# First mixer's modulation parts as column-tiled matmuls, gate row applied at the PSUM banks, negated attention scores

## The chip, the cores and the metric

The kernel runs on one core of a Trainium2 chip. The metric is the device time of one execution in microseconds (us), taken as the median of the runs. All inputs are fp32 and the result is held to fp32 accuracy. In this text PE is the matmul engine (TensorE), DVE is VectorE, ACT is ScalarE, POOL is GpSimd, and SP is the queue that issues the loads.

## What is computed

A trunk of two layers over 512 tokens of width 1024. Layer 0 mixes tokens with an mLSTM in chunks of 128 tokens, layer 1 with differential attention (8 heads, two score maps each). After each mixer comes a mixture of experts (16 experts, 2 chosen per token). Six modulation vectors per layer, `mod`, scale, shift and gate both halves:

```python
c_act = jax.nn.silu(c)
for l in range(DEPTH):
    mod = (c_act @ w_ada[l] + b_ada[l])[:, None, :]
    sh1, sc1, g1, sh2, sc2, g2 = jnp.split(mod, 6, axis=-1)
    h = _rms(x, norm1[l]) * (1.0 + sc1) + sh1
    y = _mlstm_mixer(h, ...) if l == 0 else _diff_attention(h, ...)
    x = x + g1 * y
    h = _rms(x, norm2[l]) * (1.0 + sc2) + sh2
    x = x + g2 * _grouped_moe(h, ...)

# inside _diff_attention, for a block of 128 queries
p = jax.nn.softmax(jnp.where(mask, q @ k.T * 64 ** -0.5, -jnp.inf), axis=-1)
a = p[:, :, 0] - lam * p[:, :, 1]

# at the end of either mixer: y = o @ w_out
```

## The kernel before

**Products.** A big product is three matmuls: the weight block is split into a rounded high part (ACT copy, L228) and the low part that is left (subtraction, L229), the activations likewise, and high x high, high x low and low x high are added in one PSUM bank. `split` puts the low part on VectorE. Only the strips named `qk0` (first strip of layer 0) and `b00` (first strip of layer 1) put it on GpSimd, by the last argument at the call in `strip`. Low parts live in two buffers.

**Modulation parts.** A part (l, j) is the product of the 1024 values of `cact` with a 1024x1024 block of `w_ada`, loaded as four chunks of 1 MB into the four buffers "raw", which the mixer's weights use too. Layer 0's parts 0 and 1 are made at the start by `ada_half` (matmuls, L326). During mixer 0 the six parts (0,2) to (0,5), (1,0) and (1,1) are made by `ada` off the matmul engine: ACT or VectorE scales the two halves of a chunk by the channel's value (L255, L257, L259), GpSimd adds what ACT scaled into the accumulator `acc` (L260), and at the end of a part `column_sums` turns the accumulator by eight transposes (L301), VectorE sums over the turned rows (L302) and adds the bias (L307). During mixer 1 the four parts (1,2) to (1,5) are made by `ada_rows`: four small matmuls per chunk, each with the channel values in one column of a 32-column group, side by side in one bank (L280, the tile `rowada`), evacuated into `acc` by ACT for a part's first chunk (L284) and by VectorE for the others (L286), and summed over rows by four narrow matmuls at the end of a part (`row_sums`, L312). An fp32 matmul is recorded as two.

**Output projection.** `out_proj` runs at the end of each mixer in two halves of two tokens' tiles (128 tokens each). For half 0 the four banks `po` are multiplied by the gate row `grow` (L499) and then added to the tokens `x` (L500). While half 0 runs, GpSimd multiplies each block of the still loaded weights `wo` by the gate row (L512), after its split, so that half 1 splits gated weights and only adds (L500).

**Attention.** Per block, head and map: scores `s` (L917); VectorE adds the mask and takes the row maximum (L920); VectorE multiplies that by -0.125 (L923); ACT takes exp(0.125 s - 0.125 max) with its sum (L924). Then reciprocals, the factor with lambda (L928), a scaling of the second map (L929), an addition to the first (L930), transposes `aT` (L939), and the product with v (L949). The normed rows `qrow` and `orow` come from VectorE (L891 to L897, L964) and are turned on the matmul engine (`qkT` L903, `oT` L976).

**Order.** Functions put steps off by `later`, and the framework's scheduler then orders the instructions of each engine on a modelled timeline, except those that `ordered` keeps in program order. Every engine works its list in order, and SP issues the loads in its own. `normed_T` squares a token tile at the start of a layer (ACT, L373), and VectorE (L366) and GpSimd (L367) make 1/rms from it. L1616 is the last addition of the experts' output to a token tile.

## Time and profile before

| what | value |
| --- | --- |
| median of 3 runs | 1228.6 us (1227.84 to 1230.41) |
| profiled execution, its own time | 1225.23 us |
| its span in the trace | 1223.4 us |
| mean granted matmul clock of it | 0.952 of full speed |
| busy: PE, DVE, ACT, POOL | 92%, 66%, 54%, 25% of the span |
| moved by DMA | 320.81 MB, 262 GB/s over the span |

The profiled execution is one run, 3.4 us below the median; some 2 us of its time lie outside the span. Mixer 0 takes about 30 to 285 us of the span, the experts of layer 0 up to some 580, mixer 1 up to some 920, the experts of layer 1 the rest. A window row lists, for a stretch, how long each engine was busy and in brackets how many instructions it had there, then the granted clock (1.00 is full speed, 0.50 half of it), the share of the DMA engines' time that was busy and the rate. A timeline row has the start, the duration, engine, line, operation and operands; "x8" means that eight instructions are merged, and square brackets give the idle time of the engine just before and what ended it. A matmul's duration is longer than the distance to the next matmul's start, since matmuls are pipelined, so costs on PE are read from start to start.

### The profile page before, as it was taken

The page shows a single profiled execution, that of the slowest core. Times are in us where ns is not written, and L with a number is a line of the kernel's source. Part 1 is how long each engine was busy: PE and PEld are TensorE (multiplying, and loading weights), DVE is VectorE, ACT ScalarE, POOL GpSimd, SP SyncE. Part 2 cuts the span into 40 slices and gives each one's busy share as a digit, 9 for nine tenths or more (in the row PEclk, how much of TensorE's full clock was granted, in tenths as well). Part 3 has the DMA queues.
Part 4 walks back from the last instruction along what each step waited for, and adds up shares of the span by engine and source line. Part 5 has one row for each costly group of instructions (what it writes and reads, how often), then busy time and mean ns, then how long its engine had stood idle before and what let it go on. Part 6 is the DMA issues. An engine that isn't in the chain of part 4 may idle for free.

```text
span 1223.4 us, 17320 instructions
## 1 busy us (share of the span) xinstructions
PE 1126.9 (92%) x5954; PEld 816.0 (67%) x5954; DVE 808.9 (66%) x1617; ACT 659.1 (54%) x1118; POOL 307.7 (25%) x245
## 2 busy tenths in 40 slices
PE   5999999988999999996899999978797999999976
PEld 3677777777787875332897877757586787774322
DVE  4566878887888995006856566675677899893024
ACT  3456675443788885112655555555553888883110
POOL 2555482462211111101211021223233211111100
PEclk8999999997999999998999999988896999999998
DMA  9788662195799999999124444411275899999994
GB/s 345 267 284 302 230 216 104 59 346 194 280 383 382 386 380 368 398 408 370 37 70 141 138 169 138 173 69 74 99 280 193 316 386 385 377 380 372 396 414 182
DMA packets 104172, 320.81 MB, mean 262 GB/s; under 512 B 12673, under 2 KB 25097, under 8 KB 103056
## 3 DMA queue, kind: packets, MB, share of 16 engines
q1 hardware_dynamic: 95120, 298.67, 65.8%
q0 software_dynamic: 8960, 20.99, 4.7%
q8 instruction: 49, 0.80, 0.3%
q14 instruction: 43, 0.35, 0.1%
HBM read 309.66 MB, written 20.97 MB: 270 GB/s over the span
## 4 chain that ended last, share of the span: by engine, by line
PE 70%; DMA 12%; DVE 11%; ACT 4%; issue 2%; POOL 1%; SPq 0%; DVEq 0%; POOLq 0%; ACTq 0%
PE pge L237 8%; PE pue L237 8%; PE pge L1339 6%; PE po L237 6%; DMA we<-in_moe_w_gu_dram 5%; DMA ada<-in_w_ada_dram 5%; PE py0e L237 4%; PE py1e L237 4%; PE pye L1366 3%; PE s L917 3%; PE pcf L1398 2%; PE o L949 2%; PE xTe L427 1%; PE rowada L280 1%; PE psr L1087 1%
## 5 line engine op out<-in xcount | busy, mean ns | idle before, releaser
L1339 PE MATMUL pge<-we,xfe 128*64 128x512 f32 x448 | 106.3, 616 | 19.2 <-DMA we<-in_moe_w_gu_dram 19.2
L260 POOL TENSOR_TENSOR acc<-acc,ada 128x1024 f32<-128x1024 f32 x30 | 80.8, 2694 | 54.8 <-ACT ada L259 22.2
L1348 DVE TENSOR_TENSOR acte<-acte,pge 128x256 f32<-128x256 f32 x14 | 5.9, 421 | 119.3 <-ACT acte L1347 119.3
L1311 POOL DMA_INDIRECT xg<-h2d,lstd x26 | 26.8, 1031 | 223.0 <-PE xTe L427 152.5
L1339 PEld LDWEIGHTS pge<-we,xfe 128*64 128x64 f32 x448 | 30.4, 141 | 74.4 <-issue 51.1
L367 POOL TENSOR_TENSOR qrs<-qrs,nhalf 128x4 f32<-128x4 f32 x32 | 35.5, 1111 | 154.9 <-DVE qrs L366 126.5
L1366 PE MATMUL pye<-we,aTe 128*64 128x512 f32 x224 | 50.6, 593 | 1.1 <-ACT aTe L1355 1.1
L259 ACT ACTIVATE ada<-ada,cact 128x1024 f32<-128x1024 f32 x30 | 33.8, 1145 | 31.0 <-DMA ada<-in_w_ada_dram 31.0
L924 ACT ACTIVATE p<-p,mx 128x128 f32<-128x128 f32 (+3 forms) x64 | 35.7, 559 | 23.7 <-DVE mx L923 23.6
L920 DVE CUSTOM_DVE_ANT_0 p<-s,maskW 128x128 f32<-128x128 f32 (+3 forms) x64 | 30.4, 487 | 26.6 <-ACT orow L951 14.3
L512 POOL TENSOR_TENSOR wo<-wo,grow 128x1024 f32<-128x1024 f32 x16 | 40.9, 2573 | 23.6 <-DVE wos102l L229 15.8
L1347 ACT ACTIVATE acte<-pge 128x256 f32<-128x256 f32 x14 | 5.4, 383 | 73.1 <-PE pge L1339 73.1
L917 PE MATMUL s<-kTb,qTb 64*128 64x128 f32 (+3 forms) x128 | 40.1, 503 | 2.9 <-DVE mx L920 2.2
L1366 PEld LDWEIGHTS pye<-we,aTe 128*64 128x64 f32 x224 | 16.0, 137 | 32.3 <-issue 29.6
L427 PE MATMUL xTe<-ident,xg 128*128 128x128 f32 x144 | 23.0, 290 | 5.8 <-POOL we L220 3.2
L1463 POOL DMA_INDIRECT yd<-yoe,lstd x12 | 14.7, 1227 | 52.0 <-ACT yoe L1558 51.3
L949 PE MATMUL o<-vb,aTs 128*128 128x128 f32 x160 | 26.1, 303 | 0.7 <-ACT aTs L941 0.7
L1378 ACT ACTIVATE yo<-pye,twins 128x512 f32<-128x512 f32 x8 | 5.5, 687 | 38.9 <-PE pye L1366 38.9
L367 POOL TENSOR_TENSOR ors<-ors,nhalf 128x2 f32<-128x2 f32 (+1 forms) x12 | 11.2, 930 | 58.8 <-DVE mx L923 39.5
L949 PEld LDWEIGHTS o<-vb,aTs 128*128 128x128 f32 x160 | 23.2, 214 | 3.0 <-ACT aTs L941 1.6
L1379 POOL DMA_INDIRECT yd<-yo,rows x8 | 8.0, 1001 | 65.7 <-ACT yo L1378 65.4
L427 PEld LDWEIGHTS xTe<-ident,xg 128*128 128x128 f32 x144 | 18.5, 149 | 8.2 <-issue 6.0
(2557 smaller groups left out, 3871.5 us busy)
## 6 DMA issues: line engine op xcount, KB each, us to landing
we<-in_moe_w_gu_dram SPq DMA_DIRECT2D x128, 1024.0 KB, 8.7
we<-in_moe_w_down_dram SPq DMA_DIRECT2D x64, 1024.0 KB, 8.9
ada<-in_w_ada_dram SPq DMA_DIRECT2D x48, 1024.0 KB, 5.5
we<-yd SPq DMA_DIRECT2D x8, 1024.0 KB, 18.3
wo<-in_a_w_out_dram SPq DMA_DIRECT2D x4, 1024.0 KB, 4.9
wo<-in_b_w_out_dram SPq DMA_DIRECT2D x4, 1024.0 KB, 4.9
x<-in_x_dram SPq DMA_DIRECT2D x4, 512.0 KB, 5.0
qk0w<-in_a_w_in_dram SPq DMA_DIRECT2D x2, 1024.0 KB, 14.7
```

What stands on the lines that cost most here:

```text
L237: T.matmul(ps, (xh, xh, xl)[i], w, start=first and i == 0, stop=last and i == 2)
L259: A.activation(raw[:, k], raw[:, k], AF.Copy, scale=cact[:, kt:kt + 1])
L260: G.tensor_tensor(acc, acc, raw[:, k], op=ALU.add)
L367: pows.append(G.tensor_tensor(r, r, nhalf[:, 0:ncol], op=ALU.pow))
L427: T.transpose(ps[:, k * P:(k + 1) * P], row[:, kt * P:(kt + 1) * P], ident)
L512: G.tensor_tensor(raw[:, k], raw[:, k], grow, op=ALU.mult)
L917: T.matmul(ps[:, 0:n], part(qTs, h)[q0:q0 + BHD, j * P:(j + 1) * P], part(kTs, h)[q0:q0 + BHD, 0:n], start=True, stop=True)
L920: V.tensor_tensor_reduce(p[:, 0:n], ps[:, 0:n], maskW[:, S - n:S], scale=1.0, scalar=NEG, op0=ALU.add, op1=ALU.max, accum_out=mx[:, cc:cc ...
L924: A.activation(p[:, 0:n], p[:, 0:n], AF.Exp, scale=0.125, bias=mx[:, cc:cc + 1], accum_out=mx[:, 2 + cc:3 + cc])
L949: T.matmul(po[:, 0:P], aT[:, kb * P:(kb + 1) * P], part(vs, h)[:, kb * P:(kb + 1) * P], start=kb == 0, stop=kb == j)
L1339: T.matmul(pgu[hf * CS:(hf + 1) * CS].rearrange("p (g c) -> p g c", g=2), x[:, kt], w[:, :, hf], start=kt == 0, stop=kt == NK - 1))
L1366: T.matmul(py[hf * CS:(hf + 1) * CS], aT[:, k, ch * CS:(ch + 1) * CS], w[:, 0, hf * 512:(hf + 1) * 512], start=ch + k == 0, stop=ch + k == 2))
```

## The change

- All of layer 0's later parts are made by `ada_rows`. `ada`, `column_sums` and `ada_sums` are gone, and one accumulator tile per layer serves all parts of that layer.
- The low parts of `qk0` and `b00` are made on VectorE like the others.
- The gate row is applied at the banks in both halves. The multiplication of the loaded weights on GpSimd is gone.
- The factor -0.125 goes into the column that scales the queries. The mask has the opposite sign, VectorE takes a minimum, exp gets scale -1, the separate multiplication of the extremum is gone, and the scaling and addition of the two maps are one instruction.
- The 1/rms of token tiles 2 and 3 at the start of layer 1 is issued after the last addition before it (`added`), and the last additions are kept in program order.

```diff
-    loads, last, act_last = [], [], []
+    loads, last, act_last, added = [], [], [], []
...
-    def ada(l, j):
...
-            for k in range(2):
-                kt = ch * 2 + k
-                if kt == 0:
-                    A.activation(acc, raw[:, k], AF.Copy, scale=cact[:, kt:kt + 1])
-                elif k == 0 and l == 0:
-                    V.scalar_tensor_tensor(acc, raw[:, k], cact[:, kt:kt + 1], acc, op0=ALU.mult, op1=ALU.add)
-                else:
-                    A.activation(raw[:, k], raw[:, k], AF.Copy, scale=cact[:, kt:kt + 1])
-                    G.tensor_tensor(acc, acc, raw[:, k], op=ALU.add)
...
     def ada_rows(l, j):
 
-        if j == 2:
+        if (l, j) in ((0, 2), (1, 2)):
             both[:] = [room[0].tile([P, D], F32, tag="acc", name=f"acc{l}{j}", bufs=room[1])]
...
-    def column_sums(dst, accs, name):
...
-    def ada_sums(l, j, acc):
...
     def modulation_parts(l):
...
-            yield from (ada_rows if l else ada)(i, j)
+            yield from ada_rows(i, j)
...
-        r = rstd_of(ss, 1, D, f"r{l}{t}")
+        with tc.issue_after(added[0].ins) if added and t > 1 else nullcontext():
+            r = rstd_of(ss, 1, D, f"r{l}{t}")
...
-                yield k0 + k, split(raw[:, k:k + a], a, n, f"{name}s{k0 + k}", G if name in ("qk0", "b00") else V)
+                yield k0 + k, split(raw[:, k:k + a], a, n, f"{name}s{k0 + k}")
...
-                    if half == 0:
-                        V.tensor_tensor(ps[t, n], ps[t, n], grow[:, cols], op=ALU.mult)
+                    V.tensor_tensor(ps[t, n], ps[t, n], grow[:, cols], op=ALU.mult)
                     V.tensor_tensor(xt[t][:, cols], xt[t][:, cols], ps[t, n], op=ALU.add)
...
-                if half == 0:
-                    G.tensor_tensor(raw[:, k], raw[:, k], grow, op=ALU.mult)
...
+            if nm == "q":
+                V.tensor_scalar(wc, wc, -0.125, None, op0=ALU.mult)
...
-            V.tensor_scalar(maskW[:, S - P:], maskW[:, S - P:], 0.0, NEG, op0=ALU.is_gt, op1=ALU.mult)
+            V.tensor_scalar(maskW[:, S - P:], maskW[:, S - P:], 0.0, -NEG, op0=ALU.is_gt, op1=ALU.mult)
...
-                    V.tensor_tensor_reduce(p[:, 0:n], ps[:, 0:n], maskW[:, S - n:S], scale=1.0, scalar=NEG,
-                                           op0=ALU.add, op1=ALU.max, accum_out=mx[:, cc:cc + 1])
+                    V.tensor_tensor_reduce(p[:, 0:n], ps[:, 0:n], maskW[:, S - n:S], scale=1.0, scalar=-NEG,
+                                           op0=ALU.add, op1=ALU.min, accum_out=mx[:, cc:cc + 1])
                     pr.append(p)
-                    V.tensor_scalar(mx[:, cc:cc + 1], mx[:, cc:cc + 1], -0.125, None, op0=ALU.mult)
-                    A.activation(p[:, 0:n], p[:, 0:n], AF.Exp, scale=0.125, bias=mx[:, cc:cc + 1],
+                    A.activation(p[:, 0:n], p[:, 0:n], AF.Exp, scale=-1.0, bias=mx[:, cc:cc + 1],
                                  accum_out=mx[:, 2 + cc:3 + cc])
...
-                V.tensor_scalar(p1[:, 0:n], p1[:, 0:n], mx[:, 5:6], None, op0=ALU.mult)
-                V.tensor_tensor(p0[:, 0:n], p0[:, 0:n], p1[:, 0:n], op=ALU.add)
+                V.scalar_tensor_tensor(p0[:, 0:n], p1[:, 0:n], mx[:, 5:6], p0[:, 0:n], op0=ALU.mult, op1=ALU.add)
...
-                        V.tensor_tensor(x, x, banks[t][hf], op=ALU.add)
+                        added[:] = [V.tensor_tensor(x, x, banks[t][hf], op=ALU.add)]
+                        ordered(added[0])
```

The matmul engine's list in the first strip of mixer 0, before. The tiles `qk0p` are that strip's banks, `psg` is the product for the gates, and `psada` the row sums of the parts made at the start:

```order
L479 MATMUL qk0p3_314<-ah0_139,qk0s2h_375 128x512
L480 MATMUL qk0p3_314<-al0_141,qk0s2h_375 128x512
L481 MATMUL qk0p3_314<-ah0_139,qk0s2l_376 128x512
L338 MATMUL psada01_403<-ones_f_95,row001_373 128x1 x4
L338 MATMUL psada01_403<-ones_f_95,row011_358 128x1 x4
L576 MATMUL psg_628<-ah0_139,wg_505 16x512
```

The same place after the change:

```order
L446 MATMUL qk0p3_314<-ah0_139,qk0s2h_375 128x512
L447 MATMUL qk0p3_314<-al0_141,qk0s2h_375 128x512
L448 MATMUL qk0p3_314<-ah0_139,qk0s2l_376 128x512
L304 MATMUL psada01_403<-ones_f_95,row001_373 128x1 x4
L304 MATMUL psada01_403<-ones_f_95,row011_358 128x1 x4
L259 MATMUL rowada020_544<-ada020_461,acc02_458 32x512 x4
L259 MATMUL rowada021_580<-ada021_495,acc02_458 32x512 x4
L446 MATMUL qk0p0_311<-ah1_140,qk0s4h_430 128x512
```

Two chunks of part (0,2) now stand between the matmuls of the strip; 22 more chunks stand between the matmuls from here to the beginning of the output projection.

VectorE's list at the end of layer 0's output projection, half 1, before. `po020` and `po021` are the banks of token tile 2, `po030` and `po031` those of tile 3, `guse00l` and `guse01l` low parts of the first expert's weights:

```order
L229 TENSOR_TENSOR guse00l_2665<-we0_1980,guse00h_2664 128x1024
L500 TENSOR_TENSOR x2_86<-x2_86,po020_2239 128x512
L500 TENSOR_TENSOR x2_86<-x2_86,po021_2240 128x512
L500 TENSOR_TENSOR x3_89<-x3_89,po030_2241 128x512
L229 TENSOR_TENSOR guse01l_2669<-we0_1980,guse01h_2668 128x1024
L500 TENSOR_TENSOR x3_89<-x3_89,po031_2242 128x512
```

The same place after the change:

```order
L229 TENSOR_TENSOR guse00l_2677<-we0_1996,guse00h_2676 128x1024
L465 TENSOR_TENSOR po020_2247<-po020_2247,grow0_1922 128x512
L465 TENSOR_TENSOR po021_2248<-po021_2248,grow0_1922 128x512
L466 TENSOR_TENSOR x2_86<-x2_86,po020_2247 128x512
L465 TENSOR_TENSOR po030_2249<-po030_2249,grow0_1922 128x512
L229 TENSOR_TENSOR guse01l_2681<-we0_1996,guse01h_2680 128x1024
L465 TENSOR_TENSOR po031_2250<-po031_2250,grow0_1922 128x512
L466 TENSOR_TENSOR x2_86<-x2_86,po021_2248 128x512
L466 TENSOR_TENSOR x3_89<-x3_89,po030_2249 128x512
L466 TENSOR_TENSOR x3_89<-x3_89,po031_2250 128x512
```

Four multiplications stand among the four additions, and three of the additions, one of them tile 2's second, now stand behind the low part `guse01l`.

VectorE's list at the start of layer 1, before. `ss` is a token tile's sum of squares, `r` its 1/rms, and `pcf` holds the experts' output:

```order
L366 TENSOR_SCALAR r11_5172<-ss11_5170 128x1
L1616 TENSOR_TENSOR x2_86<-x2_86,pcf20_5079 128x512
L1616 TENSOR_TENSOR x2_86<-x2_86,pcf21_5080 128x512
L366 TENSOR_SCALAR r12_5206<-ss12_5204 128x1
L1616 TENSOR_TENSOR x3_89<-x3_89,pcf30_5089 128x512
L1616 TENSOR_TENSOR x3_89<-x3_89,pcf31_5090 128x512
```

The same place after the change:

```order
L332 TENSOR_SCALAR r11_5184<-ss11_5182 128x1
L1580 TENSOR_TENSOR x2_86<-x2_86,pcf20_5091 128x512
L1580 TENSOR_TENSOR x2_86<-x2_86,pcf21_5092 128x512
L1580 TENSOR_TENSOR x3_89<-x3_89,pcf30_5101 128x512
L1580 TENSOR_TENSOR x3_89<-x3_89,pcf31_5102 128x512
L332 TENSOR_SCALAR r12_5218<-ss12_5216 128x1
```

The first step of tile 2's 1/rms now stands behind the two additions to tile 3.

## Rows read from the trace of the kernel before

**Rows 1.** The page: busy time and share of the span of the matmul engine

```profile
PE 1126.9 (92%) x5954; PEld 816.0 (67%) x5954; DVE 808.9 (66%) x1617; ACT 659.1 (54%) x1118; POOL 307.7 (25%) x245
```

**Rows 2.** Windows: stretch, length, busy time (instructions) per engine, clock, DMA share, GB/s

```profile
100.00:120.00 20.00, 19.12 (x88) 14.93 (x87) 13.94 (x18) 10.66 (x12) 10.26 (x5) 1.00 0.84 289
...
240.00:260.00 20.00, 13.50 (x67) 10.41 (x67) 19.93 (x22) 6.41 (x10) 17.48 (x8) 0.91 1.00 401
...
340.00:360.00 20.00, 20.00 (x93) 16.04 (x93) 18.31 (x18) 17.11 (x20) 2.85 (x3) 1.00 1.01 387
...
600.00:800.00 200.00, 199.17 (x1488) 164.06 (x1486) 126.24 (x482) 107.93 (x297) 38.80 (x36) 1.00 0.39 132
```

**Rows 3.** Timeline of PE in mixer 0: start us, duration us, line, operands

```profile
39.39 0.39 PE L479 MATMUL qk0p<-ah,qk0s2h 128*128 128x512 f32 x1
39.71 1.06 PE L326 MATMUL rowada<-ada,cpad 128*32 128x512 f32 x8
40.70 0.50 PE L480 MATMUL qk0p<-al,qk0s2h 128*128 128x512 f32 x1
```

**Rows 4.** Groups by line, PE: count, duration ns min/median/max, first and last start

```profile
L301 PE MATMUL psada<-ident,acc x48: 270/273/308, 80.2 to 238.3; 128*128 128x128 f32 x48
...
L312 PE MATMUL psada<-halves,acc x32: 165/252/372, 694.5 to 833.4; 128*128 128x2 f32 x32
```

**Rows 5.** The page's groups: count, busy us, mean ns, idle time before

```profile
L260 POOL TENSOR_TENSOR acc<-acc,ada 128x1024 f32<-128x1024 f32 x30 | 80.8, 2694 | 54.8 <-ACT ada L259 22.2
...
L512 POOL TENSOR_TENSOR wo<-wo,grow 128x1024 f32<-128x1024 f32 x16 | 40.9, 2573 | 23.6 <-DVE wos102l L229 15.8
```

**Rows 6.** Waits of PE, 40 to 240 us: total us, times, longest

```profile
PE n L704 <- DVE core L736: 2.6, 3, 1.6
PE v1p L455 <- DVE v1s2l L229: 1.1, 1, 1.1
PE qk1p L479 <- ACT qT L649: 0.8, 1, 0.8
PE psgT L585 <- DVE cs L302: 0.8, 1, 0.8
```

**Rows 7.** Waits of PE, 240 to 275 us

```profile
PE psrow L360 <- DVE swr L1030: 3.7, 1, 3.7
PE ht L427 <- DVE cs L302: 2.1, 1, 2.1
PE po L237 <- DVE wos010l L229: 0.7, 1, 0.7
```

**Rows 8.** Timeline of DVE: one low part in mixer 0, one in half 1

```profile
140.68 3.43 DVE L229 TENSOR_TENSOR v1s2l<-v1w,v1s2h 128x1024 fp32r<-128x1024 f32 x1
...
278.32 1.23 DVE L229 TENSOR_TENSOR wos017l<-wo,wos017h 128x1024 fp32r<-128x1024 f32 x1 [1.00 <-PE po L237]
```

**Rows 9.** Timeline of DVE and PE at half 1's end in layer 0

```profile
282.47 1.88 DVE L500 TENSOR_TENSOR x<-x,po 128x512 f32<-128x512 f32 x3 [0.60 <-PE po L237]
284.27 1.33 DVE L229 TENSOR_TENSOR guse01l<-we,guse01h 128x1024 fp32r<-128x1024 f32 x1
...
286.26 1.09 PE L1075 MATMUL x2T<-ident,x 128*128 128x128 f32 x8 [1.49 <-DVE x L500]
```

**Rows 10.** Timeline of DVE at the start of layer 1

```profile
582.22 0.15 DVE L366 TENSOR_SCALAR r<-ss 128x1 f32<-128x1 f32 x1 [1.27 <-ACT sq L373]
```

**Rows 11.** Waits of PE, 800 to 900 us

```profile
PE qkT L903 <- DVE mx L928: 4.7, 1, 4.7
PE oT L976 <- ACT o L978: 3.9, 3, 1.4
PE s L917 <- DVE mx L920: 2.2, 1, 2.2
PE aT L939 <- ACT o L978: 2.0, 1, 2.0
```

**Rows 12.** Timeline of POOL and DVE before two of these waits

```profile
814.11 5.24 POOL L512 TENSOR_TENSOR wo<-wo,grow 128x1024 f32<-128x1024 f32 x2
...
814.59 2.56 DVE L891 TENSOR_TENSOR qrow<-qrow,qrs 128x256 f32<-128x256 f32 x1
...
860.60 2.40 DVE L928 SCALAR_TENSOR_TENSOR mx<-mx,nlam 128x1 f32<-128x1 f32 x1
```

**Rows 13.** Window behind the last of these waits

```profile
864.50:871.33 6.83, 6.83 (x21) 3.97 (x20) 3.11 (x15) 4.59 (x17) 0.00 (x0) 0.50 0.01 4
```

More of the change, by code (lines that the diff above doesn't have):

```diff
@@ L243, in trunk @@
     mod = const.tile([P, 2, 6, NK], F32, name="mod")
-    def ada(l, j):
-        if room[2]:
-            room[2].pop()()
-        acc = room[0].tile([P, D], F32, tag="acc", name=f"acc{l}{j}", bufs=room[1])
-        for ch in range(4):
-            raw = load(wk(w_ada[l, ch * 256:(ch + 1) * 256, j * D:(j + 1) * D]), 2, D, f"ada{l}{j}{ch}")
-            for k in range(2):
-                kt = ch * 2 + k
-                if kt == 0:
-                    A.activation(acc, raw[:, k], AF.Copy, scale=cact[:, kt:kt + 1])
-                elif k == 0 and l == 0:
-                    V.scalar_tensor_tensor(acc, raw[:, k], cact[:, kt:kt + 1], acc, op0=ALU.mult, op1=ALU.add)
-                else:
-                    A.activation(raw[:, k], raw[:, k], AF.Copy, scale=cact[:, kt:kt + 1])
-                    G.tensor_tensor(acc, acc, raw[:, k], op=ALU.add)
-            if ch == 3:
-                room[2].append(lambda: ada_sums(l, j, acc))
-                later(3, lambda: room[2] and room[2].pop()())
-            yield
     def ada_rows(l, j):
-        if j == 2:
+        if (l, j) in ((0, 2), (1, 2)):
             both[:] = [room[0].tile([P, D], F32, tag="acc", name=f"acc{l}{j}", bufs=room[1])]
@@ L294, in ada_rows @@
             yield
-    def column_sums(dst, accs, name):
-        for i, acc in enumerate(accs):
-            ps = t_tile(f"{name}{i}")
-            for k in range(4):
-                T.transpose(ps[:, k * P:(k + 1) * P], acc[:, k * P:(k + 1) * P], ident)
-            V.tensor_reduce(dst[:, i], ps.rearrange("p (k n) -> p k n", k=4), axis=AX.X, op=ALU.add)
-    def ada_sums(l, j, acc):
-        cs = small.tile([P, 2, 4], F32, tag="cs", name=f"cs{l}{j}", bufs=2)
-        column_sums(cs, (acc[:, 0:512], acc[:, 512:]), f"psada{l}{j}")
-        V.tensor_tensor(mod[:, l, j], cs.rearrange("p a k -> p (a k)"), badc[:, l, j], op=ALU.add)
     def row_sums(l, j, acc):
```

## Prediction

> **What bounds the kernel now.** The page comes first, to see which engine is nearly always busy: the matmul engine, 92% of the span, with no other above two thirds [rows 1]. That is a mean over stages, so the windows by stage come next [rows 2]. Three kinds of stage are to be seen. In the body of mixer 0 (100 to 120 us is typical) PE is busy 19.12 of 20 us at the full granted clock, while VectorE and GpSimd are not full and the DMA engines have room. In the body of mixer 1 (600 to 800 us) PE is busy 199.17 of 200 us. In the experts (340 to 360 us) the DMA engines are full at 387 GB/s; their transfers start when the mixer in front has let its buffers go, so a mixer that ends later moves everything behind it by as much. The fourth kind is the exception: the ends of the two mixers, such as 240 to 260 us, where PE is busy only 13.50 us, VectorE 19.93 and GpSimd 17.48.
>
> Then come the waits of PE, to see who ends its idle time: in the body of mixer 0 all that is listed is small [rows 6], at the start of the output projection [rows 7] and at the end of attention [rows 11] single waits of 2 to 5 us stand. Last, the timeline around these, to see why the engine named was late [rows 8, 12].
>
> So the question is simple: the change takes work from GpSimd, ACT and VectorE, which wait, and gives the largest piece to PE, which doesn't. Against that stand the places where GpSimd's work holds up VectorE and through it PE.
>
> **Part 1: layer 0's parts by matmuls.** Removed are the additions on GpSimd (80.8 us busy [rows 5]), the scalings on ACT and VectorE, and the 48 transposes. Added are 6 x 4 = 24 chunks of eight matmul records each, their evacuations, and six row sums. The price of a chunk on PE is in the trace, since the start-up uses the same form: in the middle of the qk0 strip a run of eight starts at 39.71 and the next matmul at 40.70, so 0.99 us, while the strip's own matmuls around it start without a break [rows 3]. The record's own 1.06 us includes the pipelined end. I take 1.05, between them: 24 x 1.05 = **25.2 us**, all in stages where PE has no idle time to put it in. The row sums are 6 x 8 = 48 short records against 48 transposes [rows 4], each about as long as the other (252 against 273 ns): nothing, within 1 us either way. The evacuations (24 of them) are far fewer than the removed scalings and turned sums on the same two engines, and lie beside matmuls in a window where VectorE is busy 13.94 and ACT 10.66 of 20 us; I cost them at nothing. If that cover failed, a late evacuation holds its bank and with it the next chunk, some tenths of a us each; 0 to 3 us in all goes into the range.
>
> What comes back in the body of mixer 0 is at most the waits that depend on VectorE or ACT. The low part v1s2l took 3.43 us while GpSimd was adding, another low part of the same size with GpSimd idle 1.23 us [rows 8]; its wait (1.1) goes, the one on the turned sums (0.8) goes since these are removed, and of the 2.6 on `core` and the 0.8 on qT I give back half [rows 6], with about 0.9 from smaller ones like them: together **-4.5 us** (0 to -7).
>
> The Trainium skill ("SBUF — State Buffer", section "SBUF: two separate sides") says that VectorE and GpSimd lock a shared pair of ports for a whole instruction and the loser blocks. The trace agrees with the 3.43 against 1.23 us, and the rule would make GpSimd's removed work a gain for VectorE; it says nothing of PE, where this sum is made.
>
> **Part 2: gate row at the banks.** It removes 16 multiplications on GpSimd, 40.9 us [rows 5], and adds two multiplications for each of the two tokens' tiles in half 1, four per layer.
>
> At layer 0's output projection GpSimd is in a row of eight of these while the waits of 3.7, 2.1 and 0.7 us stand [rows 7]. The first two hang on VectorE steps that are late in the same stretch where VectorE is busy 19.93 of 20 us. With GpSimd quiet, and the turned sums gone, I take all 6.5 us as gone, and 1 us more because the clock falls for a while behind them (0.91 on average in that window [rows 2]): **-7.5 us** (-3 to -9). What is late next there is PE itself.
>
> At the end of attention the same thing is seen more sharply. From 814.11 GpSimd does two multiplications, and the step on `qrow` that starts on VectorE in that time lasts 2.56 us; PE waits 4.7 us for this chain. The step on `mx` at 860.60 lasts 2.40 us, with waits of 2.2 and 2.0 us around it [rows 11, 12]. Without GpSimd these steps cost some tenths, so I take 4.2 of the 4.7 and 4.0 of the 4.2. Behind the last wait the granted clock is at 0.50 (1.2 GHz) for 6.83 us with PE busy all through [rows 13]; at 2.4 GHz that work takes half, -3.4. Together 11.6. The `oT` waits (3.9 us) come from a chain between ACT and PE that the change does not touch, and stay; and a step that is no longer late may show another behind it, so I take **-10 us** (-5 to -13).
>
> The price stands at the end of half 1. Before, the last addition to tile 3 is behind three additions and a low part, all on VectorE without a break from 282.47, and PE already waits 1.49 us for it [rows 9]. Four multiplications of about 0.62 us each (an addition's share of the 1.88 us for three) join the list ahead of it; none has idle time to go into, except where a bank is finished early. 4 x 0.62 = 2.5 per layer, **+5 us** for both (0 to +7), since the router and all experts are behind these tiles.
>
> **Part 3: the rest.** At the start of layer 1 the 1/rms of tile 2 waited 1.27 us for the square on ACT with tile 3's additions queued behind it [rows 10]; afterwards they go first. That is **-1 us** (-2.5 to 0, the end of the chain being the square of tile 3). The low parts of qk0 and b00 on VectorE are six instructions of 1.23 us [rows 8] in places where VectorE waits for loads or matmuls: nothing (-1 to +1). The fewer steps per score map shorten VectorE's list, but between 600 and 800 us PE is busy 199.17 of 200 us [rows 2], so there is nothing to give back: 0 (-1 to 0; at the end of attention it is in the -10).
>
> **The sum**, against the profiled execution: +25.2 - 4.5 - 7.5 - 10 + 5 - 1 = **+7.2 us**, 1225.2 to 1232.4. That execution lies 3.4 us below the median of three; the same difference on the median gives 1228.6 + 7.2 = 1235.8, rounded **1236 us**. With the terms off by a few us in either direction: 1230 to 1242.
>
> **The rivals.**
>
> 1. *Faster: the waits at the mixers' ends go as a whole.* One mechanism: GpSimd's multiplications are what makes VectorE late, and without them PE runs through. Then go 7 us in the body, 9 in layer 0's projection, and in attention all four waits (12.8) with three low-clock stretches like the one at 864.5 (about 3.4, 1.7 and 1.7), so 19.6; the banks' multiplications cost 1 per layer. 25.2 - 7 - 9 - 19.6 + 2 - 1 = -9.4, **1219 us**. It decides from gains of 25.2 + 2 on. For it: three of the four engines lose work. Against: the `oT` waits hang on ACT. Chance 0.14.
> 2. *Faster: PE has room.* If a busy share of 96 to 100% overstates PE because matmuls are pipelined, chunks slip in between others. By the weight loads, busy 14.93 of 20 us [rows 2], 5.07 us would be free there, and the chunks need about 2.5 (25.2 over some 200 us); part 1 then costs nothing and the total is 7.2 - 25.2 = -18, **1211 us**. Against it stands the start of the next matmul, moved by the full 0.99 us [rows 3]. Chance 0.07. The Trainium skill ("Perfetto Trace Analysis", section "Identifying the Most-Contended Engine") holds matmul busy time to be no measure of headroom and points to the weight loads' busy share instead, which speaks for this rival.
>
> 3. *A wash.* Gains as in the forecast's better halves (-5, -8, -12), and the tail costs 2: 25.2 - 25 + 2 - 1 = +1, **1230 us**. Chance 0.14.
> 4. *Slower still: VectorE and the raw buffers become the bound.* A chunk now keeps its raw buffer until PE's ordered place for it, and the next strip's load on SP is queued behind; with four buffers, a chunk that waits some us for PE makes a strip's weights late. If that costs 0.5 us for each of 16 chunks of the body, and the gains are at their low ends (-2, -5, -7), the total is 25.2 + 8 - 14 + 5 = +24, **1253 us**. For it: loads took their place in a mixer whose DMA share is already 0.84 [rows 2]. Chance 0.10.
>
> That the change doesn't do what it says is no case with a chance of its own: the order shows the chunks in PE's list and the GpSimd steps gone.
>
> **Chances.** Forecast 0.55, rivals 0.14, 0.07, 0.14 and 0.10. About 0.2% (2.5 us) is what a measurement of this kernel can tell from no change, so same is 1226.1 to 1231.1. Faster: rivals 1 and 2, 0.21. Same: rival 3 and a corner of the forecast, 0.16. Slower: the rest, 0.63. For 8 in 10 the range takes in the forecast and the wash, reaches down into rival 1, half of it, and up into the beginning of rival 4: 1219 to 1247.
>
> **What the next profile would show.** Right: eight-record groups `rowada` some 1.05 us apart from the next matmul in 40 to 240 us, mixer 0 ending some 13 to 18 us later (25.2 - 4.5 - 7.5 + 2.5 = +15.7 when the experts of layer 0 begin), mixer 1 shorter by 6 to 10, no GpSimd multiplication at 234 or 814 us, VectorE's steps there at tenths of a us, PE's wait for `x` at the end of half 1 grown from 1.5 to about 4 us. Wrong: mixer 0 ending less than 10 us later (PE had room, or the stalls were worth more than listed), new waits of PE on DMA for strips (rival 4), or the clock at 0.50 around 816 to 871 us as before although GpSimd is quiet, which would mean that the `oT` chain sets that stretch.

## The result

The changed kernel takes 1243.97 us (median, 1238.86 to 1247.11), the kernel before 1229.47 us beside it. The ratio is 1.0115, with a 95% interval of 1.0075 to 1.0155: slower by 14.5 us. The direction was forecast, and the time lies in the range of 1219 to 1247; the amount is twice the +7.2 of the sum, so that the median lies 8 us above the 1236 that was forecast and outside its narrower 1230 to 1242. The profiled execution took 1245.97 us (span 1244.0), 2.0 above its median, while the one of before lies 4.2 below its own. So the two traces differ by 20.7 us where the medians differ by 14.5, and some 6 us of that is the spread of single executions. More on the spread below.

The page of the changed kernel, busy time and share of each engine, answering to [rows 1]:

```profile
PE 1160.9 (93%) x6146; PEld 822.8 (66%) x6146; DVE 741.8 (60%) x1532; ACT 628.5 (51%) x1092; POOL 169.8 (14%) x193
```

VectorE lost 67 us of work, GpSimd 138 and ACT 31; PE gained 34. The windows of the changed kernel, columns as in [rows 2]:

```profile
100.00:120.00 20.00, 20.00 (x100) 13.76 (x100) 7.76 (x12) 6.30 (x8) 0.00 (x0) 1.00 0.62 210
260.00:280.00 20.00, 18.07 (x95) 14.33 (x93) 15.17 (x23) 9.62 (x13) 6.62 (x6) 1.00 1.03 419
```

The body of mixer 0 is now PE from end to end. The start of the output projection, which lies some 20 us later, is no longer a hole: 18.07 busy where 13.50 were. A chunk, on PE's timeline, answering to [rows 3]:

```profile
99.79 0.39 PE L423 MATMUL v0p<-v0s2h,al 128*128 128x512 f32 x1
100.11 1.06 PE L259 MATMUL rowada<-ada,acc 128*32 128x512 f32 x8
101.11 0.50 PE L421 MATMUL v0p<-v0s2h,ah 128*128 128x512 f32 x1
```

1.00 us from start to start. Over layer 0's 192 records, each taken to the start of the matmul behind it, this sums to 26.2 us, 1.09 per chunk, with one wait of 0.4 us in it.

To see where the 20 us of the trace arise, I follow four points of the program. The first matmul of the first expert in layer 0 and in layer 1 (the two times in the first row), and the first matmul of mixer 1 (the first time in the second), before:

```profile
L237 PE MATMUL pge<-guse00h,xh0e x2: 793/794/794, 310.1 to 945.0; 128*128 128x512 f32 x2
...
L454 PE MATMUL b00p<-b00s0h,bh x16: 277/282/421, 588.3 to 602.3; 128*128 128x256 f32 x16
```

and after:

```profile
L237 PE MATMUL pge<-guse00h,xh0e x2: 793/794/794, 328.0 to 962.1; 128*128 128x512 f32 x2
...
L421 PE MATMUL b00p<-b00s0h,bh x16: 277/282/582, 608.3 to 622.0; 128*128 128x256 f32 x16
```

| point | later by (us) | forecast |
| --- | --- | --- |
| first expert, layer 0 | 17.9 | 15.7 |
| mixer 1 begins | 20.0 | 14.7 |
| first expert, layer 1 | 17.1 | 7.2 |
| end of the span | 20.6 | 7.2 |

Mixer 0 is off by two. Mixer 1 was to become 7.5 us shorter and is 2.9 shorter, which is below the 6 to 10 that the prediction named as a sign of being right. The rest is missing behind both mixers, where the experts were taken as merely shifted. The waits of PE at the end of mixer 1 (815 to 945 us), columns as in [rows 11], with `x2T` for the turned token tiles:

```profile
PE oT L940 <- ACT o L942: 3.8, 3, 1.5
PE x2T L1039 <- DVE x L466: 3.5, 2, 3.0
```

The same wait for the token tile in the kernel before (797 to 925 us):

```profile
PE x2T L1075 <- DVE x L500: 1.5, 1, 1.5
```

All three waits that the forecast took as gone are gone (4.7 + 2.2 + 2.0), the `oT` waits stand as forecast, and the wait for the token tile has grown from 1.5 to 3.5. Of the low clock at the end of attention, 27.3 us in four stretches between 816 and 878 us before, 13.7 remain: 10.2 at the `oT` waits (846.16 to 856.40) and 3.4 (887.12 to 890.53). So a sign that the prediction named for being wrong came true for the stretch at the `oT` chain, but most of the gain arrived. It was given back by what comes after it. VectorE's timeline at that place in the changed kernel, answering to [rows 9], which show the same place of layer 0:

```profile
928.55 1.23 DVE L229 TENSOR_TENSOR guse00l<-we,guse00h 128x1024 fp32r<-128x1024 f32 x1 [1.10 <-PE po L237]
930.37 1.30 DVE L465 TENSOR_TENSOR po<-po,grow 128x512 f32<-128x512 f32 x2 [0.59 <-PE po L237]
931.58 0.68 DVE L466 TENSOR_TENSOR x<-x,po 128x512 f32<-128x512 f32 x1
932.17 0.69 DVE L465 TENSOR_TENSOR po<-po,grow 128x512 f32<-128x512 f32 x1
932.77 1.91 DVE L229 TENSOR_TENSOR guse01l<-we,guse01h 128x1024 fp32r<-128x1024 f32 x1
934.61 0.68 DVE L465 TENSOR_TENSOR po<-po,grow 128x512 f32<-128x512 f32 x1
935.21 1.86 DVE L466 TENSOR_TENSOR x<-x,po 128x512 f32<-128x512 f32 x3
```

From 930.37 to 937.07 there is no break. Of tile 2 the second half and of tile 3 everything is finished behind a low part that belongs to the experts. By the order of the list the first of the last three additions is tile 2's second half, and it is this that PE waits 3.0 us for: PE goes on at 935.94, and tile 3 costs it no wait any more. Within the wait, at 934.90, its granted clock falls to 1.2 GHz (0.50). Windows of the low clock at this place, changed kernel and kernel before:

```profile
934.90:969.04 34.14, 26.18 (x114) 23.36 (x115) 23.94 (x95) 9.88 (x16) 9.10 (x10) 0.50 0.37 135
```

```profile
925.94:946.42 20.48, 13.75 (x65) 12.76 (x66) 14.61 (x76) 3.90 (x6) 6.85 (x7) 0.50 0.38 142
```

Before, PE is back at 2.4 GHz 1.4 us after the first expert's first matmul (946.42 against 945.0); now 6.9 us after it (969.04 against 962.1). The experts' first matmuls run at the low clock in between.

### The profile page after: what moved, and what is told of

Read it like the earlier page. It is cut to its first block, busy times and chain, and to the rows that moved or that the text cites. A ratio compares the mean times of both kernels' runs of the same rounds, so it can differ in the third digit from the quotient of the medians.

```text
span 1244.0 us, 17483 instructions
## 1 busy us (share of the span) xinstructions
PE 1160.9 (93%) x6146; PEld 822.8 (66%) x6146; DVE 741.8 (60%) x1532; ACT 628.5 (51%) x1092; POOL 169.8 (14%) x193
## 4 chain that ended last, share of the span: by engine, by line
PE 80%; DMA 8%; DVE 7%; ACT 2%; issue 1%; POOL 1%; SPq 0%; DVEq 0%; POOLq 0%; ACTq 0%
PE pge L237 8%; PE pue L237 8%; PE po L237 7%; PE pge L1303 6%; PE py0e L237 4%; PE py1e L237 4%; PE rowada L259 3%; DMA we<-in_moe_w_gu_dram 3%; PE pye L1330 3%; PE s L883 2%; DMA b00w<-in_b_w_in_dram 2%; PE pcf L1362 1%; PE xTe L394 1%; PE o L913 1%; DMA ada<-in_w_ada_dram 1%; PE psr L1051 1%
## 5 line engine op out<-in xcount | busy, mean ns | idle before, releaser
L1303 PE MATMUL pge<-we,xfe 128*64 128x512 f32 x448 | 106.7, 618 | 19.9 <-DMA we<-in_moe_w_gu_dram 19.9
L259 PE MATMUL rowada<-ada,acc 128*32 128x512 f32 x320 | 45.5, 604 | 0.4 <-PE psada L304 0.2
L265 DVE TENSOR_TENSOR acc<-acc,rowada 128x512 f32<-128x512 f32 x30 | 20.5, 684 | 22.8 <-PE rowada L259 22.8
L333 POOL TENSOR_TENSOR rs<-rs,nhalf 128x2 f32<-128x2 f32 x8 | 5.6, 696 | 193.0 <-DVE rs L332 184.5
L913 PE MATMUL o<-vb,aTs 128*128 128x128 f32 x160 | 24.2, 287 | 1.2 <-ACT aTs L905 1.2
L1362 PE MATMUL pcf<-yo,self 64*128 64x512 f32 x96 | 21.7, 598 | 2.3 <-DVE yo L1336 2.3
L915 ACT ACTIVATE orow<-o,mx 128x128 f32<-128x128 f32 x32 | 11.3, 362 | 23.3 <-PE o L913 23.3
## 6 DMA issues: line engine op xcount, KB each, us to landing
qk0w<-in_a_w_in_dram SPq DMA_DIRECT2D x2, 1024.0 KB, 14.7
```

The source lines that it names most:

```text
L259: T.matmul(ps[at:at + 32], cp[:, ch * 2 + k], raw[:, k, hf * 512:(hf + 1) * 512], start=True, stop=True)
L333: pows.append(G.tensor_tensor(r, r, nhalf[:, 0:ncol], op=ALU.pow))
L913: T.matmul(po[:, 0:P], aT[:, kb * P:(kb + 1) * P], part(vs, h)[:, kb * P:(kb + 1) * P], start=kb == 0, stop=kb == j)
L1303: T.matmul(pgu[hf * CS:(hf + 1) * CS].rearrange("p (g c) -> p g c", g=2), x[:, kt], w[:, :, hf], start=kt == 0, stop=kt == NK - 1))
L1362: ordered(T.matmul(banks[hf], sel[at, t], yo[at], start=first, stop=last))
```

## The experiments

Eleven kernels ran, for three questions: what the parts cost (1, 2, 4), what the gate row gains and gives back (3, 5 to 8), and which version is better than both kernels (4, 7, 9 to 11). Every ratio is against runs of the kernel before on the same chip, whose median was 1228.3 to 1228.7 us.

**1. The parts alone.** The kernel before, with only this:

```diff
-        if j == 2:
+        if (l, j) in ((0, 2), (1, 2)):
...
-            yield from (ada_rows if l else ada)(i, j)
+            yield from ada_rows(i, j)
```

> The kernel before, with layer 0's six later modulation parts made as column-tiled matmuls and nothing else changed. Theory (PE is full, chunks are paid in full): 24 chunks at the 1.09 us that the changed kernel shows, +26, less 4 to 8 us for waits of PE on VectorE that go in the body of mixer 0 with GpSimd's additions: 1247 to 1251 us against 1229.5. Rival (PE has room, or the additions on GpSimd were a large hidden cost): below 1240 us. Layer 1 should be as before, within 2 us.

Measured: 1248.17 us, ratio 1.0159 (1.0132 to 1.0187), +19.9 us. The first expert of layer 0 starts 22.1 us later and layer 1 adds nothing, since the one of layer 1 starts 21.9 later:

```profile
L237 PE MATMUL pge<-guse00h,xh0e x2: 792/792/792, 332.2 to 966.9; 128*128 128x512 f32 x2
```

Of the waits in 40 to 240 us this is the whole list (7.6 us before, its larger ones in [rows 6]):

```profile
PE rowada L280 <- PE psada L338: 0.9, 1, 0.9
PE s L685 <- ACT core L707: 0.6, 1, 0.6
PE qk0p L480 <- DVE wck L834: 0.3, 1, 0.3
PE ht L427 <- DVE h2l L430: 0.3, 1, 0.3
```

PE was full, and it pays for the chunks in full. GpSimd's additions were hidden but for the 5.5 us of waits that are gone. In the projection of layer 0, where GpSimd still multiplies the weights, the waits did not go with the parts and their turned sums. They are one wait now (240 to 330 us; the 5.3 us end at 276 us, the other 1.5 stand at the end of half 1 as before), against 6.5 in [rows 7]:

```profile
PE x2T L1075 <- DVE x L500: 6.8, 2, 5.3
```

**2. Half of the parts.** As in 1, for three of the six parts:

```diff
-        if j == 2:
+        if (l, j) in ((0, 5), (1, 2)):
...
-            yield from (ada_rows if l else ada)(i, j)
+            yield from (ada_rows if l or (i, j) in ((0, 5), (1, 0), (1, 1)) else ada)(i, j)
```

> The kernel before with three of layer 0's six later modulation parts, (0,5), (1,0) and (1,1), made as column-tiled matmuls, 12 chunks, and the other three as before; nothing else. Theory (a chunk is paid in full wherever it stands): half of what all six cost, 12 x 1.09 = 13 less some 2 to 4 us of waits, so 1237 to 1240 us against 1228.3. Rival (there is room on PE for some chunks and the last ones are the dear ones, or the first ones): below 1233 or above 1244 us.

Measured: 1240.09 us, ratio 1.0096 (1.0059 to 1.0133), +11.8. Twelve chunks cost 11.8 where twenty-four cost 19.9; half of that lies inside the interval. No room shows up for the first ones, and the last are not dearer within this interval.

**3. The gate row at the banks alone.** The kernel before, with this:

```diff
-                    if half == 0:
-                        V.tensor_tensor(ps[t, n], ps[t, n], grow[:, cols], op=ALU.mult)
+                    V.tensor_tensor(ps[t, n], ps[t, n], grow[:, cols], op=ALU.mult)
...
-                if half == 0:
-                    G.tensor_tensor(raw[:, k], raw[:, k], grow, op=ALU.mult)
```

> The kernel before with the gate row applied at the banks in both halves and the multiplication of the weights on GpSimd gone; nothing else changed. Theory (the negated scores, the low parts of the first strips and the order at the start of layer 1 are worth 1 us together): within 2 us of the run that has all of the change but the parts, so 1220 to 1224 us. Rival (those small edits carry a gain or a loss of their own): 4 us or more away from it.

Measured: 1220.47 us, ratio 0.9938 (0.9919 to 0.9957), -7.8 us. Its waits of PE between 790 and 930 us, the two longest in sum:

```profile
PE oT L973 <- ACT o L975: 3.8, 3, 1.4
PE x2T L1072 <- DVE x L499: 3.5, 2, 3.0
```

These head the list as in the changed kernel, with neither the parts nor the other edits in it: the waits of 4.7, 2.2 and 2.0 were GpSimd's multiplications, and the longer wait for `x` is the multiplications at the banks. The same points as above:

```profile
L237 PE MATMUL pge<-guse00h,xh0e x2: 793/793/793, 305.0 to 935.5; 128*128 128x512 f32 x2
```

5.1 us earlier in layer 0 (forecast -7.5 + 2.5 = -5.0) and 9.5 in layer 1 (forecast -5.0 - 10 + 2.5 = -12.5). The end is only 6.3 earlier (span 1217.1), so some 3 us are lost in the experts behind mixer 1.

**4. Everything but the parts.** The changed kernel, with the first hunk of its diff taken back.

> The changed kernel with layer 0's six later modulation parts made off the matmul engine as in the kernel before; everything else of the change stays. Theory: the gate row at the banks gains 7 to 8 us in layer 0's projection and 9 to 10 at the end of attention, and loses some 10 at the two ends of half 1 and in the clock behind them, the start of layer 1 gives 1: 1219 to 1223 us, so faster than both kernels. Rival (the ends of half 1 take back all that the waits gave): 1228 to 1231 us. If the parts cost less than thought, this lies near the changed kernel's 1244.

Measured: 1219.80 us, ratio 0.9924 (0.9897 to 0.9951), -8.5 us. The parts are thus worth 24.2 us on top of the rest of the change, against 19.9 by themselves, a difference that lies inside the intervals. The rest without them beats the kernel before. The two runs that hold the gate row, 3 and 4, are equal within their intervals.

**5. The eight multiplications left out.** The changed kernel, with the banks of half 1 not multiplied, so that tokens 256 to 511 get an ungated mixer output:

```diff
-                    V.tensor_tensor(ps[t, n], ps[t, n], grow[:, cols], op=ALU.mult)
+                    if half == 0:
+                        V.tensor_tensor(ps[t, n], ps[t, n], grow[:, cols], op=ALU.mult)
```

> The changed kernel with the gate row left out in half 1 of the output projection, in both layers, so that tokens 256 to 511 get an ungated mixer output; the eight multiplications are gone and all else stays. Theory (the ends of half 1 cost the wait itself and then the low clock behind it): the wait of PE for the token tile is back at about 1.5 us, the low clock behind mixer 1 is as short as before (some 20 us in place of 34), and the time falls by 8 to 12 us to 1232 to 1236. Rival (only the wait counts): it falls by 4 to 5 us to 1239 or 1240. Rival (the clock behind the mixers has nothing to do with it): it falls by under 2 us.

Measured: 1231.87 us, ratio 1.0020 (1.0004 to 1.0035), so 12.1 us less than the changed kernel (11.7 by the ratios, whose intervals leave some 6 to 17). Its trace holds the same instructions of the engines as the changed kernel's but for these eight, so that the ungated tokens brought no other work. The wait for the token tile in layer 1, the window of the low clock behind it, and the points of the program:

```profile
PE x2T L1040 <- DVE x L467: 1.5, 1, 1.5
```

```profile
934.61:955.09 20.48, 13.74 (x64) 11.63 (x63) 14.78 (x72) 3.90 (x6) 6.46 (x7) 0.50 0.40 145
```

```profile
L237 PE MATMUL pge<-guse00h,xh0e x2: 793/794/796, 325.4 to 952.8; 128*128 128x512 f32 x2
...
L421 PE MATMUL b00p<-b00s0h,bh x16: 278/281/582, 603.4 to 617.5; 128*128 128x256 f32 x16
```

In layer 1 the wait and the low clock are as in the kernel before, and the clock is back 2.3 us after the first expert's first matmul instead of 6.9. Against the changed kernel's trace the four points are earlier by 2.6, 4.9, 9.3 and 13.0 us. So the ends of half 1 cost 2.6 and, counted over all of mixer 1, 4.4 (9.3 - 4.9) up to the first expert, and the experts behind it cost another 2.3 and 3.7. Eight instructions of 0.69 us, 5.5 us of work, are worth some 12.

**6. The experts' low part behind the additions.** The gate row alone (run 3), with this, where `ends` holds the last addition and `issue_after` puts an instruction behind another one:

```diff
-        ready = [split(fetch.ready[0][:, k:k + 1], 1, D, f"guse0{k}") for k in range(2)]
+        ready = []
+        for k in range(2):
+            with tc.issue_after(ends[0].ins) if k else nullcontext():
+                ready.append(split(fetch.ready[0][:, k:k + 1], 1, D, f"guse0{k}"))
```

> The kernel before with the gate row at the banks in both halves, and VectorE's low part of the first expert's second weight block (guse01) queued behind the last addition of half 1; nothing else. Theory (VectorE's unbroken list at the end of half 1 delays the token tiles, and the low clock behind it follows from the waits): that low part is 1.3 to 1.9 us of the list, so the wait for tile 3 falls by that in each layer, and 3 to 6 us in all come off the 1220.5 us of the run with the gate row alone: 1214 to 1217 us. Rival (what ends last there is the squares and the choice of experts behind the token tile, and the clock is low anyway): within 1.5 us of 1220.5.

Measured: 1217.93 us (1208.79 to 1224.00), ratio 0.9899 (0.9858 to 0.9939). 2.5 us below run 3, between the theory and the rival, and the intervals overlap: the time alone doesn't decide. The wait did fall, from 3.0 us at its longest to 1.1, less than the 1.5 of the kernel before, but the low clock behind it stayed. Waits of PE between 880 and 940 us, and the window of the low clock:

```profile
PE x2T L1073 <- DVE x L500: 2.1, 3, 1.1
```

```profile
910.24:940.96 30.72, 24.78 (x111) 22.17 (x110) 23.79 (x93) 9.04 (x16) 10.07 (x10) 0.50 0.41 151
```

It ends 6.6 us behind the first expert's first matmul (934.4 us), so it does not follow from the length of this one wait. Yet it goes with the multiplications. In each of the four traces without them in half 1 (the kernel before and runs 1, 2 and 5) the stretch behind mixer 1 is 20.5 us long, in the nine with them 23.9 to 34.1. And where it ends more than 6 us behind the first expert's first matmul (the changed kernel, runs 3, 6, 8 and 11), layer 1's experts take 281.0 to 281.9 us from there to the end of the span; in the other eight traces 278.2 to 280.7.

**7. Tile 2 first.** Run 6, and in half 1 each multiplication is followed by its own addition:

```diff
-                    V.tensor_tensor(ps[t, n], ps[t, n], grow[:, cols], op=ALU.mult)
-                    ends[:] = [V.tensor_tensor(xt[t][:, cols], xt[t][:, cols], ps[t, n], op=ALU.add)]
+                    with tc.issue_after(ends[0].ins) if half and ends else nullcontext():
+                        V.tensor_tensor(ps[t, n], ps[t, n], grow[:, cols], op=ALU.mult)
+                        add = V.tensor_tensor(xt[t][:, cols], xt[t][:, cols], ps[t, n], op=ALU.add)
+                    if half:
+                        ends[:] = [add]
```

> As the run with the queued low part, and in half 1 each bank's multiplication is followed by its own addition, tile 2 before tile 3. Theory: tile 2 is done after four steps instead of seven, so its turns fill the time in which tile 3 is finished; another 1 to 3 us off, 1212 to 1216 us. Rival (tile 3 sets the end whatever the order): equal to that run within 1 us. A multiplication that waits for its bank now holds up the additions behind it, which could cost up to 1 us per layer.

Measured: 1214.24 us (1208.78 to 1220.71), ratio 0.9872 (0.9833 to 0.9910), 14 us below the kernel before and not told apart from run 6. Its VectorE timeline at the end of mixer 1:

```profile
907.24 0.70 DVE L500 TENSOR_TENSOR po<-po,grow 128x512 f32<-128x512 f32 x1 [0.59 <-PE po L238]
907.98 0.69 DVE L501 TENSOR_TENSOR x<-x,po 128x512 f32<-128x512 f32 x1
...
912.04 0.68 DVE L501 TENSOR_TENSOR x<-x,po 128x512 f32<-128x512 f32 x1
912.63 2.33 DVE L230 TENSOR_TENSOR guse01l<-we,guse01h 128x1024 fp32r<-128x1024 f32 x1
```

The last addition ends 5.5 us after the first multiplication starts, instead of 6.7 in the changed kernel. In layer 0 the saving on the wait was lost: the list of waits between 230 and 330 us now begins with a wait for `hot`, the one-hot rows of the experts' choice. This run, and the kernel before:

```profile
PE psl L1146 <- DVE hot L1145: 4.5, 2, 3.5
```

```profile
PE psl L1145 <- DVE hot L1144: 1.0, 1, 1.0
```

**8. The changed kernel with that end.** Both edits of runs 6 and 7 on the changed kernel.

> The changed kernel with only the end of half 1 reordered, as in the run with the chained additions. Theory (the end of half 1 is what the sum undersized, and a part of it is the order of VectorE's list): 4 to 7 us less than the changed kernel's 1244.0, so 1237 to 1240 us; what stays above the kernel before is then the matmul parts. Rival (the multiplications themselves cost it, in whatever order): 1242 us or more.

Measured: 1239.54 us, ratio 1.0080 (1.0050 to 1.0110), 4.4 us below the changed kernel, in the theory's range. But the intervals of the two overlap, so that a part of the price is the order of the list is likely and not shown. Most of the price remains; with all eight multiplications left out it was 12.1. In layer 0 this trace has run 7's wait for `hot` too, 4.0 us long.

**9. Run 4 with the first strips' low parts back on GpSimd.**

```diff
-                yield k0 + k, split(raw[:, k:k + a], a, n, f"{name}s{k0 + k}")
+                yield k0 + k, split(raw[:, k:k + a], a, n, f"{name}s{k0 + k}", G if name in ("qk0", "b00") else V)
```

> The changed kernel without the parts by matmul (as the earlier run so called) and with the low parts of the first strips of both layers back on GpSimd; gate row at the banks, negated scores and the order at the start of layer 1 stay. Theory (the trace of the earlier run is 4 us behind the kernel before at 80 us and 2 us more behind at the start of layer 1, so the low parts on VectorE cost there when VectorE also makes the modulation parts): 3 to 5 us less than the earlier run's 1219.8, so 1215 to 1217 us. Rival (those offsets are given back later): 1219 to 1221 us.

Measured: 1216.33 us, ratio 0.9891 (0.9859 to 0.9923), 3.5 us below run 4, with intervals that overlap. The traces show a place for it. Waits of PE between 30 and 130 us in run 4, and in this run:

```profile
PE qk1p L480 <- ACT qT L647: 3.0, 2, 2.4
```

```profile
PE qk1p L480 <- ACT qT L647: 0.7, 1, 0.7
```

So the low parts on VectorE likely cost a few us when VectorE also makes the modulation parts. With the parts on PE this cost is not seen: there the list of waits between 40 and 260 us begins with this one:

```profile
PE s L649 <- ACT core L671: 0.8, 1, 0.8
```

**10. All that gained.** Run 9 with the end of half 1 from run 7.

> The gate row at the banks, the negated scores and the order at the start of layer 1 from the change; modulation parts and low parts of the first strips as in the kernel before; and, new, the end of half 1 in the order of the run with the chained additions (tile 2 first, the first expert's low part behind). Theory (the gains add up): the 1216.3 us of the run without parts and low parts, less the 4 to 6 us that the new end gave on the gate alone: 1210 to 1213 us, the fastest of all. Rival (the low clock behind the mixers takes it back): 1215 to 1217 us.

Measured: 1218.30 us (1215.19 to 1220.83), ratio 0.9910 (0.9876 to 0.9943). The gains did not add up; this one is a miss. The trace shows a new wait. VectorE's timeline at the end of mixer 0 in this run, and then PE's wait there, which was 1.0 us in the kernel before:

```profile
278.84 2.33 DVE L230 TENSOR_TENSOR guse01l<-we,guse01h 128x1024 fp32r<-128x1024 f32 x1
...
281.22 2.15 DVE L1095 SCALAR_TENSOR_TENSOR xg<-xg,re,srow 128x1024 f32<-128x1024 f32 x1
...
283.36 0.94 DVE L1146 TENSOR_SCALAR hot<-slot,pk 128x128 fp32r<-128x128 f32 x4
```

```profile
PE psl L1147 <- DVE hot L1146: 5.0, 2, 4.0
```

With tile 2 done early, its own next step (`xg`) is ready early too and goes ahead of the one-hot rows `hot` that PE needs; run 7 has the same wait (3.5). Both steps, `guse01l` and `xg`, take over 2 us here, while GpSimd multiplies two tiles `xg` (3.47 us from 278.82).

**11. All that gained, without the chain.** Run 10 with run 6's end of half 1 in place of run 7's.

> As the run that put all gains together, but the end of half 1 without the chained additions: only the first expert's second low part is queued behind the last addition. In the trace of that run the chain moved the wait: the experts' low part (2.33 us) and a step on tile 2 (2.15 us) came between the choice of experts and its one-hot rows, and the matrix engine waited 4.0 us for these where it had waited 1.0. Theory (that new wait ate the chain's gain): 1212 to 1216 us, below the 1218.3 of that run and the 1216.3 without any change to the end. Rival (these differences are below what single runs spread): 1216 to 1219 us.

Measured: 1213.07 us (1209.34 to 1215.94), ratio 0.9854 (0.9829 to 0.9878): 15.6 us below the kernel before and 31 below the changed kernel, the lowest median of the study. PE's wait for `hot` is short again:

```profile
PE psl L1144 <- DVE hot L1143: 1.0, 1, 1.0
```

The first expert of layer 0 starts 3.9 us earlier than in run 10 (302.2 against 306.1). So the chain's new wait is the likely reason for the 5.2 us between the two medians, whose intervals just touch. It is not shown: the two profiled executions have the same span, 1214.1 us, and the lead is down to 0.6 us at layer 1's first expert (932.8 against 933.4). Runs 6, 7 and 9 lie between, at 1214 to 1218 us, and are not told apart from their neighbours.

## Why the prediction was right or wrong

- **Part 1, the chunks:** right. 25.2 was summed, 26.2 measured from start to start, and the parts alone cost 22.1 us on the trace, 19.9 by the medians, where 25.2 - 4.5 = 20.7 was forecast. That PE has no room (against rival 2) is shown by runs 1 and 2, the second with half the dose at 11.8 of 19.9 us. The Trainium skill ("Perfetto Trace Analysis", section "Identifying the Most-Contended Engine") has matmul busy time as no measure of headroom; here the weight loads were busy 14.93 of 20 us [rows 2], and still every chunk was paid. What decided was the distance of starts.
- **Part 2, the projection of layer 0 and the end of attention:** right. The waits of 3.7 and 2.1 [rows 7] and of 4.7, 2.2 and 2.0 [rows 11] are gone with GpSimd's multiplications, as run 3 shows by itself; layer 0's first expert was 5.1 us earlier there, 5.0 forecast. In layer 0 the multiplications were the larger part of it: run 1, which has them but not the turned sums, still waits 5.3 us there. The low part v1s2l, 3.43 us in [rows 8], takes 1.22 in the changed kernel:

```profile
147.19 1.22 DVE L229 TENSOR_TENSOR v1s2l<-v1w,v1s2h 128x1024 fp32r<-128x1024 f32 x1
```

That 5.0 met 5.1 is partly luck. In run 3 the last matmul of layer 0's projection starts 8.8 us earlier (274.68 against 283.44; -7.5 forecast), and from there to the first expert it takes 3.7 us longer (+2.5 forecast). In mixer 1 the same two are -10.8 (-10 forecast) and +5.3 (+2.5 forecast), by these matmuls in the kernel before and in run 3:

```profile
919.72 0.39 PE L237 MATMUL po<-wos117h,o2l 128*128 128x512 f32 x1
...
904.93 0.39 PE L237 MATMUL po<-wos117h,o2l 128*128 128x512 f32 x1
```

- **Part 2, the ends of half 1: the term that was mis-sized.** The sum has +5, 2.5 per layer, as four multiplications' time. Measured are 12.1 us for the eight (run 5). The wait itself came in its size as forecast, 3.5 us against "from 1.5 to about 4", but 3.0 of it are for tile 2's second half and not, as the sum had it, for tile 3. What the step left out stands behind it. In layer 1 PE's granted clock fell 27.2 us before the first expert's first matmul (934.90 against 962.1) instead of 19.1 (925.94 against 945.0), so that the turns of tile 3 ran at 1.2 GHz too, and it rose 6.9 us behind that matmul instead of 1.4. In layer 0 it rose 6.2 us behind it instead of 1.4 (334.15 against 328.0, 311.54 against 310.1). On the trace the experts, taken as merely shifted, lost 2.1 us in layer 0 (17.9 to 20.0 later) and 3.5 in layer 1 (17.1 to 20.6). The 2.1 is no more than the spread between traces without the multiplications (277.6 us from the first expert to mixer 1 in run 1, 282.5 in run 2); the 3.5 goes with the low clock, as said at run 6. I priced the clock where a wait goes (-3.4 and -1) and not where work is added in front of the experts. With 12 in place of 5 the sum is +14, against +14.5 by the medians, closer than the intervals allow one to expect.
- **Part 3:** of the -1 at the start of layer 1 some 0.4 came. From the start of the run of matmuls that bring the experts' output together (`pcf`) to the first matmul of mixer 1 (588.3 and 608.3 us) it takes 13.6 us in the kernel before and 13.2 in the changed one:

```profile
574.69 7.14 PE L1398 MATMUL pcf<-yo,self 64*128 64x512 f32 x32 [0.85 <-DVE yo L1372]
...
595.13 7.14 PE L1362 MATMUL pcf<-yo,self 64*128 64x512 f32 x32 [1.49 <-DVE yo L1336]
```

The negated scores were put at nothing, and that stays open. Three pairs of runs differ by these and by the order at layer 1's start alone: with both, run 9 is 4.1 us below run 3 and run 11 is 4.9 below run 6, but run 10 is 4.1 above run 7. The low parts on VectorE, put at nothing, are likely worth some us without part 1, and not seen with it.

- **The range:** its upper end was set by a rival on the raw buffers that did not appear; no wait of PE on a strip's load is in the list of 40 to 260 us. The time came near that end for another reason.

Left open: why layer 0's end of half 1 is cheaper than layer 1's (2.6 against 4.4 us up to the first expert), why the low clock behind mixer 1 stays long when the wait for the token tile is short (run 6), and how much of it varies by itself.

## What to carry to other kernels

Work moved from idle engines to the one that was full cost its whole duration there, however well the form fits that engine; read its price from start to start of its neighbours, at a place where nothing waits. A helper engine that looks free can still hold up its neighbour, and it is worth taking off the few stretches where the full engine waits, which is where the gain of this change was. And work added on the last steps before a stage's end can cost more than itself: here 5.5 us of it cost some 12, with a longer wait and more of PE's low clock behind it.

## What the runs showed of the hardware

- Some steps on VectorE took 2.4 to 3.4 us while GpSimd worked on full tiles, and 0.2 to 1.2 us for the same step without that work: v1s2l 3.43 against 1.22 us, `qrow` 2.56 against 0.42, `mx` 2.40 against 0.22. Not all were held up: at 250.56 us, inside GpSimd's row of eight multiplications, a multiplication at a PSUM bank (`po`) took its usual 0.68 us.
- The clock differs from one execution of a kernel to the next, and with it the time. In run 6 the fastest execution, 1208.79 us, had a mean granted clock of 0.958 and the slowest, 1224.00 us, 0.945; in run 11 it was 0.955 at 1209.34 us and 0.946 at 1215.94. In the changed kernel's four executions it is less plain: 0.947 at 1247.11 us, but 0.954 at 1245.97 and 0.953 at 1238.86. This spread, 8 to 15 us between single executions of one kernel, is why differences of 3 us between variants could not be settled. Where in the execution the clock differs, one trace per kernel can't tell: the stretch at 1.2 GHz behind mixer 0 was 23.9 us in the kernel before and 34.1 in run 7, whose wait for the token tile was shorter and whose wait for `hot` was longer.
